# An MLP whose first quarter becomes like its others: two units of seven block products for eight, and a residual turned in four separate steps

## The chip, the core and the metric

One Trainium2 chip, one of its cores. The metric is the device time of one execution in microseconds, median of several runs; a run of the kernel before and one of the changed kernel are compared on the same chip.

## The reference

One layer of an encoder trunk on 256 tokens of width 2048, in float32: a mixer of retention and gated delta rule, a cross-attention, and an MLP of hidden width 8192. The change touches the MLP and what stands right before it:

```
x = x + cross_attention(h, mem_n, w_xq[l], w_xkv[l], w_xo[l])
h = rms_norm(x, norm_ffn_g[l])
x = x + jnp.square(jax.nn.relu(h @ w_ff1[l])) @ w_ff2[l]
return rms_norm(x, norm_final_g)
```

## The kernel before

Every large product is made of three matmuls. A float32 operand is split into a rounded part (the `whi` tiles, a cast on ScalarE, L125) and a remainder (`wlo`, a subtraction on VectorE, L126), and high by high, high by low and low by high are summed. Weights come through `fetch`: one transfer of 1 MB on SP's queue (L113) into one of three `raw` buffers, whose two halves of 1024 columns are then cast and get their remainders. The split halves live in three pairs of buffers, and every fourth half goes to a spare pair (`whx`, `wlx`) as soon as `spare` holds a pool. A scheduler sets the final order on each engine; every engine and SP's queue then run in that order.

The MLP runs in four quarters of 2048 hidden columns each (`fb`). A quarter first makes its hidden columns, eight groups (`b2`) of 256, each from two fetches of w_ff1 (numbered here 0 to 15, two to a group): 64 matmuls at L210 for a group. `evac_h` takes each group from PSUM, rectifies, squares and splits it. Then come the products with w_ff2 (L1227). A plain one takes a block of 512 by 512 weights for all 256 tokens, 24 matmuls. `with_seven` instead makes the product of 2 by 2 blocks with seven smaller products of 12 matmuls for eight: it loads the weight blocks b11, b12, b22, b21 (L1210, 1 MB each) into `rt` and `tr`, subtracts them from one another on VectorE (L1261, two halves of 1024 columns), and reads sums of hidden blocks that `token_sums` has made. Each finished product is added to the residual `res` on VectorE (L1142).

`rt` holds the residual with features on the partitions, and `res` needs it with tokens there. So VectorE transposes it in blocks of 32 by 32 into `tr` (L1124, four instructions of 1024 columns), and `place` copies it on into `res`: 32 transfers of 64 KB on SP's queue (L1131, called scatters here), in runs of 128 bytes. Each scatter needs all four transposes, and b22 and b21 can be loaded into `tr` only after all scatters.

A quarter's w_ff2 has 16 blocks of 512 by 512. Quarters two to four make eight of them as two such units of seven products (14 x 12 matmuls) and eight plain (8 x 24), and put some of the products between the last groups of hidden columns (`early`). The first makes one unit with seven (7 x 12) and twelve blocks plain (12 x 24), all of it after its hidden columns; its scatters go four to a group, all along the hidden columns. The norm ahead of the MLP has its own small matmuls (L1042); 54 matmuls of the first quarter stand before them.

Of the kernel before, what the change touches and what calls it, by code (L numbers as in the profile page):

```python
# [52 lines left out]
def trunk(ctx: ExitStack, tc: tile.TileContext, x_f, mem_f, positions, lead_f, small_f, w_in, ret_gn_g, w_out, w_xq,  # L53
# [23 lines left out]
    spare, turn = [], [0]  # L77
# [26 lines left out]
    def fetch(pieces, k, n, cuts=1, hold=None, at=(0, 0)):  # L104
# [3 lines left out]
        with tc.high_priority(offset=100000):  # L108
# [6 lines left out]
            for i in range(2):  # L115
# [1021 lines left out]
    spare.append(fp)  # L1137
# [60 lines left out]
    def with_seven(hid, rows, last, early):  # L1198
# [80 lines left out]
        if early:  # L1279
            load_block(b11, 0, 0)  # L1280
            yield
            load_block(b12, 0, 1)
            product(shared, part(0, 0), b11, "shared", (b11, b12, b11))
            read((0, 0, shared))
            yield
            load_block(b22, 1, 1)
            product(p5, summed(0), b11, "p5", (b11, b22, b11))
            read((1, 0, p5), (1, 1, p5))
            yield
            load_block(b21, 1, 0)  # L1290
            product(shared, summed(1), b11, "shared", (b12, b22, b12))
            read((1, 0, shared))
            yield
            product(shared, summed(2), b12, "shared", (b11, b21, b11))
            read((0, 1, shared), (1, 1, shared))
            if last:
                product(p5, summed(3), b22, "p3")
                read((1, 0, p5))
            yield
            for n in range(2):  # L1300
                take(n, stream_ps())
            plain(0, 2)
            load_block(b12, 0, 3)
            if last:
                final.append(quad_a().both.rearrange("p k s -> p (k s)").bitcast(F32))
                with tc.issue_after(fetched[-1]):
                    nc.sync.dma_start(final[0], norm_final_g.partition_broadcast(P))
            if not last:
                product(own[1][0], summed(3), b22, (1, 0))
            plain(0, 3)  # L1310
            load_block(b22, 1, 3)
            product(own[0][0], part(1, 0), b21, (0, 0))
            read((0, 0, own[0][0], True))
            product(own[0][1], part(1, 1), b11, (0, 1))
            read((0, 1, own[0][1], True))
            plain(1, 2)
            load_block(b11, 0, 2)
            take(2, [bank(), bank()])
            plain(2, 2)
            load_block(b21, 1, 2)  # L1320
            opened.difference_update(("shared", "p5"))
            product(shared, part(0, 0), b11, "shared", (b11, b12, b11))
            read((2, 0, shared))
            plain(1, 3)
            read(*((1, t, own[1][t], True) for t in range(NT)))
            product(p5, summed(0), b11, "p5", (b11, b22, b11))
            read((3, 0, p5), (3, 1, p5))
            plain(2, 3)
            take(3, stream_ps())
            product(own[3][0], summed(3), b22, (3, 0), (b12, b22, b12))  # L1330
            plain(3, 2)
            product(shared, summed(1), b11, "shared", (b11, b21, b11))
            read((3, 0, shared))
            if not last:
                plain(3, 3)
                read(*((3, t, own[3][t]) for t in range(NT)))
                product(own[2][0], part(1, 0), b21, (2, 0))
                read((2, 0, own[2][0]))
                product(shared, summed(2), b12, "shared")
                read((2, 1, shared), (3, 1, shared))  # L1340
                product(own[2][1], part(1, 1), b11, (2, 1))
                read((2, 1, own[2][1]))
            else:
                product(own[2][0], part(1, 0), b21, (2, 0))
                read((2, 0, own[2][0], True), (2, 1, own[2][1]))
                plain(3, 3, True)
                of_7 = parted(b12)
                with tc.issue_after(latest["lo"]), tc.issue_after(latest["hi"]):
                    add(3, 0, own[3][0])
                    of_4 = parted(b11, quad_b)  # L1350
                with tc.high_priority(offset=50000):
                    settle(3, 0)
                    latest["lo"] = latest["add"]
                    mean_square(0)
                    r_0 = factor(0)
                    finish(0, r_0, (0, 512, act, nc.sync), (1024, 1536, act, nc.sync))
                for those in unscaled:
                    scale(*those)
                read((3, 1, own[3][1]))
                product(shared, summed(2), None, "shared", halves=of_7)  # L1360
                read((3, 1, shared, True), (2, 1, shared))
                ends_of = stream_ps()
                product(ends_of, part(1, 1), None, "end", halves=of_4)
                with tc.high_priority(offset=50000):
                    with tc.issue_after(latest["square"]):
                        finish(0, r_0, (512, 1024, act, nc.sync), (1536, D, act, nc.sync))
                    junk = fp.tile([P, 2, S], F32, name="hs", tag="hs", bufs=2)
                    for c, ps in enumerate(ends_of):
                        with tc.issue_after(latest["lo"]):
                            got = add(2, 1, ps[:, :256], c * 256, c * 256 + 256)  # L1370
                        acc = ssq4[:, 1, 3 + c:4 + c]
                        vec.scalar_tensor_tensor(junk[:, c], got, 1.0, got, op0=ALU.mult, op1=ALU.mult, accum_out=acc)
                        if c:
                            vec.scalar_tensor_tensor(sums[1], acc, 1.0 / D, sums[1], op0=ALU.mult, op1=ALU.add)
                        else:
                            mean_square(1)
                    finish(1, factor(1), (0, 256, act, nc.sync), (512, 1024, vec, act), (256, 512, act, nc.sync),
                           (1024, 1536, vec, nc.sync), (1536, D, vec, act))
        else:
            for n in range(2):  # L1380
                take(n, stream_ps())
# [37 lines left out]
    for fb in range(4):  # L1419
# [5 lines left out]
        for b2 in range(8):  # L1425
# [17 lines left out]
            if early and b2 > 2:  # L1443
                next(parts_of)
# [46 lines left out]
```

## Time and profile before

| | |
|---|---|
| median of 3 runs | 2045.62 us (2044.28 to 2046.14) |
| span of the profiled execution | 2043.3 us; no other time of that execution is listed |
| TensorE busy | 2030.5 us, 99% |
| VectorE, ScalarE busy | 1550.6 us (76%), 1184.3 us (58%) |
| DMA queue of SP | 402.74 MB, 62.2% of 16 engines |

A span runs from the first instruction to the last. A wait is named by the instruction that waited and the one that released it. "DMA share" is the mean busy share of the core's 16 DMA engines; overlapping packets can bring it above 1.

### The profile page before, as it was taken

The numbers are of one execution on the slowest core, as the hardware profiler recorded it, in microseconds if no ns is written. First come the engines' busy times: TensorE is split into PE (matmuls) and PEld (weight loads), VectorE is DVE, ScalarE is ACT, GpSimd is POOL, SyncE is SP. The second block draws the span as 40 slices with busy tenths as digits, with TensorE's granted clock in tenths as the row PEclk, the third lists the DMA queues.
The fourth block names the chain that finished last, engine by engine and source line by source line (L and its number), as shares of the span: only waits on it lengthen the run. The fifth ranks groups of instructions, "written<-read, shape, count | busy, mean of one in ns | idle before, by whom it ended". The sixth has DMA issues, their size and how long they took to land.

```text
span 2043.3 us, 28453 instructions
## 1 busy us (share of the span) xinstructions
PE 2030.5 (99%) x10802; PEld 1751.4 (86%) x10802; DVE 1550.6 (76%) x2423; ACT 1184.3 (58%) x1941; POOL 38.7 (2%) x50
## 2 busy tenths in 40 slices
PE   9999999999999999999999999999999999999998
PEld 7888888988888888888888899888888888888886
DVE  5887788779667875888567666777867887888788
ACT  6655764575457554755446565555547656656655
POOL 0000000000000000000000000000000000000000
PEclk9999999999999999999999999999999999999999
DMA  9689556466555655555467655569657656665761
GB/s 329 209 259 303 184 185 197 154 189 201 180 166 183 198 190 165 186 181 190 156 212 244 191 183 163 174 180 254 221 168 234 219 163 214 201 204 166 242 231 62
DMA packets 329370, 405.24 MB, mean 198 GB/s; under 512 B 34944, under 2 KB 239632, under 8 KB 329104
## 3 DMA queue, kind: packets, MB, share of 16 engines
q1 hardware_dynamic: 328800, 402.74, 62.2%
q8 instruction: 84, 1.38, 0.3%
q10 hardware_dynamic: 432, 0.69, 0.1%
q14 instruction: 54, 0.44, 0.1%
HBM read 389.74 MB, written 11.55 MB: 196 GB/s over the span
## 4 chain that ended last, share of the span: by engine, by line
PE 97%; DVE 2%; issue 0%; DMA 0%; ACT 0%; SPq 0%; DVEq 0%; POOLq 0%; POOL 0%; ACTq 0%
PE s L210 52%; PE s L167 8%; PE s L168 8%; PE s L166 8%; PE b L1227 7%; PE s L1227 7%; PE s L400 1%; PE s L401 1%; PE s L402 1%; PE b L795 1%; PE b L698 1%; PE b L138 1%; PE b L828 1%; PE b L137 1%; PE b L139 1%
## 5 line engine op out<-in xcount | busy, mean ns | idle before, releaser
L210 PE MATMUL s<-q,whi 128*128 128x512 f32 x2816 | 969.0, 390 | 0.6 <-DVE bo L220 0.6
L126 DVE TENSOR_TENSOR wlo<-raw,whi 128x1024 fp32r<-128x1024 f32 x586 | 715.1, 1222 | 296.3 <-ACT whi L125 291.7
L125 ACT ACTIVATE whi<-raw 128x1024 fp32r<-128x1024 f32 x586 | 620.8, 1060 | 488.9 <-PE s L210 209.2
L210 PE MATMUL s<-q,wlo 128*128 128x256 f32 x2816 | 765.0, 281 | 0.0
L210 PEld LDWEIGHTS s<-q,whi 128*128 128x128 f32 x2816 | 520.6, 188 | 101.4 <-DVE bo L220 0.9
L210 PEld LDWEIGHTS s<-q,wlo 128*128 128x128 f32 x2816 | 527.2, 188 | 12.6 <-DVE wlo L126 0.5
L167 PE MATMUL s<-wlo,q 128*128 128x512 f32 x704 | 277.2, 394 | 0.0
L168 PE MATMUL s<-whi,q 128*128 128x512 f32 x704 | 274.9, 391 | 0.0
L166 PE MATMUL s<-whi,q 128*128 128x512 f32 x704 | 254.4, 391 | 0.0
L166 PEld LDWEIGHTS s<-whi,q 128*128 128x128 f32 x704 | 132.1, 188 | 27.4
L168 PEld LDWEIGHTS s<-whi,q 128*128 128x128 f32 x704 | 132.3, 188 | 26.2
L167 PEld LDWEIGHTS s<-wlo,q 128*128 128x128 f32 x704 | 132.3, 188 | 26.2
L219 ACT ACTIVATE bo<-s 128x256 f32<-128x256 f32 x192 | 73.2, 381 | 105.5 <-PE s L210 105.5
L220 DVE TENSOR_TENSOR bo<-bo,s 128x256 f32<-128x256 f32 x192 | 79.9, 416 | 43.0 <-ACT bo L219 42.8
L1227 PE MATMUL s<-whi,q 128*128 128x512 f32 x280 | 90.4, 389 | 0.0
L1250 DVE TENSOR_TENSOR wlo<-rt,whi 128x1024 fp32r<-128x1024 f32 x54 | 65.8, 1224 | 32.3 <-ACT whi L1249 31.6
L210 PE MATMUL s<-q,whx 128*128 128x512 f32 x256 | 89.2, 389 | 0.0
L125 ACT ACTIVATE whx<-raw 128x1024 fp32r<-128x1024 f32 x58 | 61.5, 1060 | 43.2 <-PE b L1227 17.2
L126 DVE TENSOR_TENSOR wlx<-raw,whx 128x1024 fp32r<-128x1024 f32 x58 | 70.9, 1222 | 17.9 <-ACT whx L125 17.4
L1249 ACT ACTIVATE whi<-rt 128x1024 fp32r<-128x1024 f32 x54 | 57.2, 1060 | 38.1 <-PE s L1227 17.8
L210 PE MATMUL s<-q,wlx 128*128 128x256 f32 x256 | 70.4, 280 | 0.0
L1227 PE MATMUL b<-whi,q 128*128 128x512 f32 x216 | 70.3, 389 | 0.0
(350 smaller groups left out, 2372.2 us busy)
## 6 DMA issues: line engine op xcount, KB each, us to landing
raw<-w_in SPq DMA_DIRECT2D x143, 1024.0 KB
raw<-w_ff SPq DMA_DIRECT2D x100, 1024.0 KB
raw<-w_xkv SPq DMA_DIRECT2D x29, 1024.0 KB
raw<-w_out SPq DMA_DIRECT2D x16, 1024.0 KB
raw<-w_xq SPq DMA_DIRECT2D x16, 1024.0 KB
raw<-w_xo SPq DMA_DIRECT2D x16, 1024.0 KB
rt<-w_ff SPq DMA_DIRECT2D x14, 1024.0 KB
tr<-w_ff SPq DMA_DIRECT2D x14, 1024.0 KB
```

The source lines that it names most:

```text
L125: latest["hi"] = act.activation(hi[:, cs], src[:, cs], AF.Copy).ins
L126: latest["lo"] = vec.tensor_sub(lo[:, cs], src[:, cs], hi[:, cs].bitcast(F32)).ins
L137: pe.matmul(o, lhs[0], rhs[0], start=first, stop=False)
L166: pe.matmul(o, xh, wh, start=first, stop=False)
L167: pe.matmul(o, xh, wl, start=False, stop=False)
L168: pe.matmul(o, xl, wh, start=False, stop=last)
L210: ins = pe.matmul(ps[b][:, :S] if part else ps[b], halves[h][part][:, i, b * P:(b + 1) * P], x[:, kk % 4, :], start=kk == 0 and not part, ...
L219: act.activation(o, ps[b][:, S:], AF.Copy)
L220: vec.tensor_add(o, o, ps[b][:, :S])
L1227: ins = pe.matmul(o, lhs[l], rhs[r], start=key not in opened, stop=last and j == 2, skip_group_check=True).ins
L1249: latest["hi"] = act.activation(hi, raw[:, c:c + 1024], AF.Copy).ins
L1250: latest["lo"] = vec.tensor_sub(lo, raw[:, c:c + 1024], hi.bitcast(F32)).ins
```

## The change

The first quarter takes the way of the others: `with_seven` loses its `early` switch and the other branch, `evac_h` rectifies and squares on ScalarE. The four transposes are put into a list, and `fetch` takes one out behind each remainder, after four empty entries. The scatters move: none in groups 0, 6 and 7, eight in groups 1 to 3, four in groups 4 and 5. The spare pair of buffers is handed out after group 0, and `sv` is then allocated before it. The long block under `if early:` only loses its indentation.

```
     fetched, steps, latest = [], [], {}
-    spare, turn = [], [0]
+    spare, turn, turns = [], [0], []
...
                     latest["lo"] = vec.tensor_sub(lo[:, cs], src[:, cs], hi[:, cs].bitcast(F32)).ins
+                if turns:
+                    turn_round_next = turns.pop(0)
+                    with tc.issue_after(latest["lo"]):
+                        turn_round_next()
...
-    for c in range(4):
+
+    def turn_round(c):
         vec.transpose(*(a[:, 4 * c:4 * c + 4, :].rearrange("p k s -> p (k s)") for a in (tr, rt)))
+
+    turns.extend(4 * [lambda: None] + [lambda c=c: turn_round(c) for c in range(4)])
...
-    spare.append(fp)
...
-    def with_seven(hid, rows, last, early):
+    def with_seven(hid, rows, last):
...
-        early = fb > 0
-        parts_of = with_seven(hid, rows, fb == 3, early)
+        parts_of = with_seven(hid, rows, fb == 3)
...
-                if early:
-                    act.activation(ps, ps, AF.Relu)
-                    act.activation(hs[:, b, :], ps, AF.Square)
-                else:
-                    vec.scalar_tensor_tensor(hs[:, b, :], ps, 0.0, ps, op0=ALU.max, op1=ALU.mult)
+                act.activation(ps, ps, AF.Relu)
+                act.activation(hs[:, b, :], ps, AF.Square)
...
-            blocks(h3, w_ff1[0], fb * D + b2 * 256, 2, evac_h, ends if early else None)
-            if early and b2 > 2:
+            blocks(h3, w_ff1[0], fb * D + b2 * 256, 2, evac_h, ends)
+            if fb == 0:
+                if b2 == 0:
+                    spare.append(fp)
+                for b8 in ((), (0, 1), (2, 3), (4, 5), (6,), (7,), (), ())[b2]:
+                    place(b8)
+            if b2 > 2:
                 next(parts_of)
-            if fb == 0:
-                place(b2)
```

On TensorE the first quarter keeps its 512 matmuls at L210, and its 372 at L1227 become 360 (L1233 in the changed kernel).

SP's queue before, from the first fetches of w_ff1 (`raw<-w_ff`, two to a group; `res<-tr` are scatters, `rt<-w_ff` loads of w_ff2 blocks):

```order
L113 DMA raw<-w_ff 128x8x256 x5
L1131 DMA res<-tr 32x16x32 x2
L113 DMA raw<-w_ff 128x8x256
L1131 DMA res<-tr 32x16x32 x3
L113 DMA raw<-w_ff 128x8x256
L1131 DMA res<-tr 32x16x32 x4
L113 DMA raw<-w_ff 128x8x256
L1131 DMA res<-tr 32x16x32 x7
L113 DMA raw<-w_ff 128x8x256 x2
L1131 DMA res<-tr 32x16x32 x4
```

Three more pairs of fetches follow, each with four scatters behind it, and only then the loads of w_ff2. The same place of the queue now:

```order
L113 DMA raw<-w_ff 128x8x256 x7
L1138 DMA res<-tr 32x16x32 x5
L113 DMA raw<-w_ff 128x8x256
L1216 DMA rt<-w_ff 128x4x512
L1138 DMA res<-tr 32x16x32 x4
L113 DMA raw<-w_ff 128x8x256
L1138 DMA res<-tr 32x16x32 x7
L113 DMA raw<-w_ff 128x8x256
L1216 DMA rt<-w_ff 128x4x512
L1138 DMA res<-tr 32x16x32 x6
L113 DMA raw<-w_ff 128x8x256
L1138 DMA res<-tr 32x16x32 x6
```

Fetch 11, four more scatters, fetch 12 and the load of b22 into `tr` come next. So the 32 scatters stand between fetch 6 and fetch 12, with the loads of b11 and b12 among them.

VectorE before, where the transposes stand (`wlo`, `wlx` are remainders of halves of weights, `n_s` is the norm):

```order
L126 TENSOR_TENSOR wlo<-raw,whi 128x1024 x2
L1044 TENSOR_SCALAR n_s<-b 128x2
L1124 STREAM_TRANSPOSE tr<-rt 128x1024 x4
L126 TENSOR_TENSOR wlx<-raw,whx 128x1024
L1115 TENSOR_TENSOR rstd3q<-n_r 128x2
```

The `wlx` there is the second half of fetch 1, which TensorE takes up behind fetch 2. And now, where `wlx` and the `wlo` after it are the two halves of fetch 3:

```order
L126 TENSOR_TENSOR wlo<-raw,whi 128x1024 x2
L1129 STREAM_TRANSPOSE tr<-rt 128x1024 x2
L1048 TENSOR_SCALAR n_s<-b 128x2
L126 TENSOR_TENSOR wlx<-raw,whx 128x1024
L1129 STREAM_TRANSPOSE tr<-rt 128x1024
L224 TENSOR_TENSOR bo<-bo,s_13013 128x256
L126 TENSOR_TENSOR wlo<-raw,whi 128x1024
L1129 STREAM_TRANSPOSE tr<-rt 128x1024
```

The four stand apart, the last one two remainders later than before.

VectorE of the changed kernel around the second of the early products (`L1256` splits b11, `L1267` subtracts b22, which is in `tr`, from it; the last row is the first remainder of fetch 12):

```order
L1256 TENSOR_TENSOR wlo<-rt,whi 128x1024
L1256 TENSOR_TENSOR wlx<-rt,whx 128x1024
L1267 TENSOR_TENSOR rt<-tr,rt 128x1024
L1148 SCALAR_TENSOR_TENSOR res<-b,rstd3q,res 128x512
L1267 TENSOR_TENSOR rt<-tr,rt 128x1024
L126 TENSOR_TENSOR wlo<-raw,whi 128x1024
```

Before, the first quarter has no such rows among its hidden columns; its products come after fetch 15.

## Rows read from the trace of the kernel before

**Rows 1.** The page: span, TensorE, and groups (busy us, mean ns, idle before).

```profile
span 2043.3 us, 28453 instructions
...
PE 2030.5 (99%) x10802; PEld 1751.4 (86%) x10802; DVE 1550.6 (76%) x2423; ACT 1184.3 (58%) x1941; POOL 38.7 (2%) x50
...
L126 DVE TENSOR_TENSOR wlo<-raw,whi 128x1024 fp32r<-128x1024 f32 x586 | 715.1, 1222 | 296.3 <-ACT whi L125 291.7
L125 ACT ACTIVATE whi<-raw 128x1024 fp32r<-128x1024 f32 x586 | 620.8, 1060 | 488.9 <-PE s L210 209.2
```

**Rows 2.** Waits of TensorE, whole span: us in total, times, longest.

```profile
PE s L210 <- DVE bo L220: 0.6, 1, 0.6
```

**Rows 3.** Timeline of TensorE: start, duration, instruction, [idle before <- releaser].

```profile
1367.93 0.28 PE L210 MATMUL s<-q,wlx 128*128 128x256 f32 x1
1368.79 0.50 PE L210 MATMUL s<-q,whi 128*128 128x512 f32 x1 [0.58 <-DVE bo L220]
```

**Rows 4.** Stretches, all engines: first quarter after the norm, second quarter.

```profile
1357.84:1522.74 164.90, 164.32 (x832) 139.87 (x832) 125.47 (x163) 82.34 (x103) 0.70 (x1) 1.00 0.74 213
1522.74:1692.74 170.00, 170.00 (x873) 145.73 (x872) 137.05 (x164) 103.63 (x144) 0.00 (x0) 1.00 0.61 196
```

**Rows 5.** Stretch, line 210 alone, third quarter: PE, PEld, PEclk, DMA, GB/s.

```profile
1693.27:1863.38 170.11, 89.13 (x512) 78.46 (x512) 1.00 0.61 198
```

**Rows 6.** Stretches, line 1227 alone, first and second quarter.

```profile
1438.30:1522.80 84.50, 84.43 (x372) 69.70 (x372) 1.00 0.52 177
1522.70:1693.00 170.30, 82.37 (x360) 67.29 (x360) 1.00 0.61 196
```

**Rows 7.** Timeline of VectorE around the transposes.

```profile
1357.67 1.22 DVE L126 TENSOR_TENSOR wlo<-raw,whi 128x1024 fp32r<-128x1024 f32 x1 [1.26 <-ACT whi L125]
...
1358.88 4.61 DVE L1124 STREAM_TRANSPOSE tr<-rt 128x1024 f32<-128x1024 f32 x4
1363.42 1.18 DVE L126 TENSOR_TENSOR wlx<-raw,whx 128x1024 fp32r<-128x1024 f32 x1
```

**Rows 8.** Groups by line in the second quarter: busy us, mean ns.

```profile
L1261 DVE TENSOR_TENSOR rt<-tr,rt 128x1024 f32<-128x1024 f32 x12 | 14.2, 1218 | 0.0
...
L1142 DVE SCALAR_TENSOR_TENSOR res<-b,rstd3q,res 128x512 f32<-128x512 f32 x13 | 9.4, 745 | 0.2 <-PE b L1227 0.2
```

**Rows 9.** Timeline of SP's queue, start and duration of issues, first quarter.

```profile
1356.44 0.37 SPq L113 DMA_DIRECT2D raw<-w_ff  x1
1363.57 1.40 SPq L1131 DMA_DIRECT2D res<-tr  x2
...
1375.21 1.08 SPq L113 DMA_DIRECT2D raw<-w_ff  x1
1376.34 8.64 SPq L1131 DMA_DIRECT2D res<-tr  x7
1385.07 1.20 SPq L113 DMA_DIRECT2D raw<-w_ff  x2
...
1393.47 3.20 SPq L113 DMA_DIRECT2D raw<-w_ff  x2
...
1411.92 2.59 SPq L113 DMA_DIRECT2D raw<-w_ff  x2
1414.56 6.90 SPq L1131 DMA_DIRECT2D res<-tr  x4
```

**Rows 10.** Stretches, all engines; the last three numbers are PEclk, DMA share, GB/s.

```profile
1381.50:1385.00 3.50, 3.50 (x21) 3.07 (x21) 1.30 (x3) 1.76 (x4) 0.00 (x0) 1.00 1.07 99
1397.50:1400.50 3.00, 3.00 (x20) 2.63 (x19) 2.97 (x7) 1.49 (x4) 0.00 (x0) 1.00 1.06 349
1413.00:1415.00 2.00, 2.00 (x13) 1.78 (x12) 0.10 (x1) 0.31 (x1) 0.00 (x0) 1.00 0.35 68
1427.00:1443.00 16.00, 16.00 (x88) 13.82 (x88) 10.69 (x17) 8.70 (x14) 0.00 (x0) 1.00 1.05 388
```

**Rows 11.** The stretch of all scatters, all engines.

```profile
1365.00:1424.00 59.00, 58.42 (x337) 51.17 (x336) 45.07 (x79) 31.26 (x49) 0.00 (x0) 1.00 1.01 232
```

**Rows 12.** The stretch after the issue of a single fetch, all engines.

```profile
1356.50:1358.00 1.50, 1.50 (x12) 1.38 (x12) 0.33 (x1) 1.06 (x1) 0.00 (x0) 1.00 0.21 58
```

**Rows 13.** Timeline of ScalarE: a cast that waited for its fetch.

```profile
1391.75 1.06 ACT L125 ACTIVATE whi<-raw 128x1024 fp32r<-128x1024 f32 x1 [4.14 <-DMA raw<-w_ff]
```

More of the change, by code (lines that the diff above doesn't have):

```diff
@@ new lines, in with_seven @@
+        load_block(b11, 0, 0)
+        yield
+        load_block(b12, 0, 1)
+        product(shared, part(0, 0), b11, "shared", (b11, b12, b11))
+        read((0, 0, shared))
+        yield
+        load_block(b22, 1, 1)
+        product(p5, summed(0), b11, "p5", (b11, b22, b11))
+        read((1, 0, p5), (1, 1, p5))
+        yield
+        load_block(b21, 1, 0)
+        product(shared, summed(1), b11, "shared", (b12, b22, b12))
+        read((1, 0, shared))
+        yield
+        product(shared, summed(2), b12, "shared", (b11, b21, b11))
@@ new lines, in with_seven @@
+        read((0, 1, shared), (1, 1, shared))
+        if last:
+            product(p5, summed(3), b22, "p3")
+            read((1, 0, p5))
+        yield
+        for n in range(2):
+            take(n, stream_ps())
+        plain(0, 2)
+        load_block(b12, 0, 3)
+        if last:
+            final.append(quad_a().both.rearrange("p k s -> p (k s)").bitcast(F32))
+            with tc.issue_after(fetched[-1]):
+                nc.sync.dma_start(final[0], norm_final_g.partition_broadcast(P))
@@ new lines, in with_seven @@
+        if not last:
+            product(own[1][0], summed(3), b22, (1, 0))
+        plain(0, 3)
+        load_block(b22, 1, 3)
+        product(own[0][0], part(1, 0), b21, (0, 0))
+        read((0, 0, own[0][0], True))
+        product(own[0][1], part(1, 1), b11, (0, 1))
+        read((0, 1, own[0][1], True))
+        plain(1, 2)
+        load_block(b11, 0, 2)
+        take(2, [bank(), bank()])
+        plain(2, 2)
+        load_block(b21, 1, 2)
+        opened.difference_update(("shared", "p5"))
@@ new lines, in with_seven @@
+        product(shared, part(0, 0), b11, "shared", (b11, b12, b11))
+        read((2, 0, shared))
+        plain(1, 3)
+        read(*((1, t, own[1][t], True) for t in range(NT)))
+        product(p5, summed(0), b11, "p5", (b11, b22, b11))
+        read((3, 0, p5), (3, 1, p5))
+        plain(2, 3)
+        take(3, stream_ps())
+        product(own[3][0], summed(3), b22, (3, 0), (b12, b22, b12))
+        plain(3, 2)
+        product(shared, summed(1), b11, "shared", (b11, b21, b11))
+        read((3, 0, shared))
@@ L1430, in evac_h @@
             def evac_h(b, ps):
-                if early:
-                    act.activation(ps, ps, AF.Relu)
-                    act.activation(hs[:, b, :], ps, AF.Square)
-                else:
-                    vec.scalar_tensor_tensor(hs[:, b, :], ps, 0.0, ps, op0=ALU.max, op1=ALU.mult)
+                act.activation(ps, ps, AF.Relu)
+                act.activation(hs[:, b, :], ps, AF.Square)
                 qh, ql = (a[:, b2 % 2 * 2 + b, :] for a in hid[-1])
```

177 lines of the change are left out of this document (44 added, 133 removed).

## The prediction, made before the change had run

> **What bounds the kernel now.** I read the page first. TensorE is busy 2030.5 of 2043.3 us [rows 1], so the question is what it does in that time and where the 13 us are. The list of waits gives one TensorE wait after the start of the kernel: 0.6 us for a PSUM evacuation [rows 2]. The timeline puts it at 1367.93, where one matmul starts 0.86 us after the one before it [rows 3]; that is in the first quarter of the MLP, which the change rewrites. Next I cut the MLP at its quarters. The second takes 170.00 us with TensorE busy for all of it; the first takes, from the norm to its end, 164.90 us, of which 0.58 idle [rows 4]. 54 of its matmuls run before the norm, at 0.174 us (89.13 us over 512 [rows 5]), so the first quarter takes 164.9 + 9.4 = 174.3 us. The granted clock is 1.00 in all of these, its 2.4 GHz level. An instruction that leaves TensorE's queue shortens the kernel, and one that arrives too late lengthens it.
>
> **What the change takes away.** The second kind of matmul (L1227) drops from 372 to 360 in the first quarter, as many as the others have. They stand at 84.43 us for 372 and 82.37 for 360 [rows 6], 2.1 us apart; 12 times 84.43/372 = 0.227 us gives 2.7. The stall at 1367.93 goes too: the half of fetch 1 that used the spare buffer waited behind the four transposes (4.61 us in one piece, its remainder after them at 1363.42 [rows 7]), so the first group of hidden columns ended late and its PSUM banks were freed late. With the spare buffer given out one group later, halves are used in their order. If the new first quarter ran like the second, it would take 170.0 us for 174.3: **-4.3 us**, of which 2.7 are the matmuls, 0.6 the stall, and 1.0 short delays and slower pairs around it.
>
> **What it adds off TensorE.** Six more halves of a weight block are cast (1.06 us on ScalarE) and get their remainder (1.222 on VectorE) [rows 1], eight more 1024-column subtractions (1.218) and six more additions into the residual (0.745) come to VectorE [rows 8], and 16 squares go from VectorE to ScalarE. VectorE: 7.3 + 9.7 + 4.5, 21.5 us, less the squares. I cost this at nothing: the second quarter has the same instructions, with VectorE busy 137.05 and ScalarE 103.63 of its 170.00 us (before, the first has 125.47 and 82.34), and TensorE has no gap there [rows 4]. Without that cover each us would count. The spare buffer also moves in SBUF, by the 2 KB of another tile; no row gives that a price, and I take nothing.
>
> **The transposes.** One by one, the fourth ends later. Up to the remainder that starts at 1357.67 the order is as before, so it ends at 1358.9; then come two transposes (1.15 each), the norm's short step, a remainder 1.2, a transpose, an addition (some 0.4), a remainder 1.2 and the last transpose [rows 7]: 1366.4, for 1363.5 before. The remainder ahead of it ends at 1365.2 and is needed by TensorE at about 1365.3, so 0 to 0.5 us; I take 0. But the 32 scatters need all four transposes, and start 2.9 us later.
>
> **The transfers.** Before, the 32 scatters lie between 1363.57 and 1421.46 on SP's queue, among eleven fetches [rows 9]. Now they lie among six, with two loads of w_ff2 squeezed in, and everything behind them on the queue waits. Prices: in 1381.5 to 1385, where nearly only scatters move, the engines are full (share 1.07) at 99 GB/s, so 65.5 KB take 0.66 us; fetches move at 349 GB/s, 1048.6 KB in 3.0; loads at 388, 2.7 [rows 10]. Check on before: 1365 to 1424 moved 232 GB/s x 59 us = 13.7 MB [rows 11]; less 32 scatters (2.10 MB) that is 11.06 fetches, so 33.2 + 21.1 = 54.3 of 59 us. 4.7 us are lost; 1.3 of them are in 1413 to 1415 (share 0.35 [rows 10]), where a fetch waited for its buffer [rows 9], and about 1 is the start. That leaves 4%.
>
> Now the queue of the changed kernel. Fetch 6 waits for the remainder that ends at 1365.2; its bytes flow 1.3 to 1.8 us after its issue (the one issued at 1356.44 had moved 87 KB by 1358.0 [rows 9, 12]); with 1.8, from 1367.1. Up to the end of fetch 11 stand six fetches, two loads and 28 scatters: 18.0 + 5.4 + 18.5 = 41.9, with 4% 43.6 us: 1410.7. Software sees it about 1.2 us later (the fetch issued at 1385.07 released ScalarE at 1391.75, and could be over at 1390 to 1391 [rows 9, 13]); cast and remainder take 1.06 + 1.22: 1414.2. TensorE, if never stopped, needs it at 1412.3: 1357.84, plus 10 matmuls of fetch 1, eight fetches of 5.53, one product of 2.75, fetch 10, and one matmul. **Stall 1.9.** Then the second product: its subtraction takes b22, whose load stands behind four more scatters and fetch 12: 1410.7 + (2.6 + 3.0 + 2.7) x 1.04 + 1.2 = 1420.5. VectorE runs in order, and the first remainder of fetch 12 stands behind that subtraction, an addition to the residual and a second subtraction: 1.22 + 0.75 + 1.22 + 1.22 = 4.4, so 1424.9; it is due at 1412.1 + 5.53 + 2.75 + 0.23 + 1.9 = 1422.5. **Stall 2.4.** Later fetches have slack, since no scatter is left and each group of columns now shares its time with a product. Sum: -4.3 + 4.3 = 0.0 on the profiled execution's span of 2043.3 us; what lies around it (the median is 2.3 us above that span) stays, so **2045.6**.
>
> With nothing lost between transfers fetch 11 ends at 1409.0 and the stalls are 0.2 and 2.1: 2043.6. With 8% lost they are 3.6 and 2.7: 2047.6.
>
> **Rivals.** (1) *The transfers are hidden.* For it: before, with the engines full for 59 us, TensorE lost only 0.58 us to a wait, and that one was not a transfer's. Against: then 58 us held eleven fetches and 32 scatters, and now 45 us must hold six, two loads and 28. No stall: 2045.6 - 4.3 = 2041.3. The same comes out if a scatter cost what its bytes cost at a load's rate, 0.17 us: 28 then take 4.7 instead of 18.5, and everything is early by 13 us. Against that stand the 99 GB/s at full share [rows 10]; I give this way 0.04 of the 0.22 below. The Trainium skill's page "DMA: Bandwidth & Descriptors", in "Why small descriptors are slow (HBM only)", says that transfers between SBUF and SBUF don't suffer from small descriptors, and that 128-byte packets still reach 78% of the link; the scatters are such transfers. By that rule the stalls would vanish; the trace disagrees.
>
> (2) *Long groups of scatters cost more; the kernel is slower.* From the fetch at 1375.21 to that at 1385.07 the queue spent 9.86 us on a fetch and seven scatters [rows 9]: 0.98 for each scatter. If the groups of 7, 6 and 6 pay that, 19 x 0.32 = 6.1 us take the place of the 1.7 lost in the sum, fetch 11 comes 4.4 us later, and nothing behind absorbs it: 2050.0. It decides from 0.97 us for a scatter in these groups (4.1 us more). Against: a cycle of two fetches and four scatters took 8.4 us (1385.07 to 1393.47), 0.6 for each.
>
> (3) *The transposes stop TensorE*: the remainder due at 1365.3 comes 1 us late or more, 2046.5 and up.
>
> **Numbers.** Chances: the forecast, 2043.6 to 2047.6, 0.54; (1) 0.22; (2) 0.18; (3) or another wait 0.06. 0.2% is 4.1 us, about what a measurement of this kernel can tell from no change. (1) lies on that bound, so I count two thirds of it as faster: 0.15; of (2) three quarters as slower, with some of (3): 0.16; same 0.69. The range takes in (1) and (2): 2041.2 to 2050.2; the forecast's own is 2043.6 to 2047.6.
>
> **What would show it.** TensorE's 360 matmuls and the lost wait at 1368 are the first step. For the second, TensorE's idle time lies where fetch 11 and fetch 12 start, some 55 and 64 us after the norm, ScalarE waiting for a transfer ahead of the first, VectorE for b22's load ahead of the second, with the share of the DMA engines near 1 from the first scatter on. No idle time there shows (1); idle time from fetch 9 on shows (2). A quarter that is longer than 170 us without idle time would show that my cover for VectorE and ScalarE, or the buffers' places, is wrong.

## The result

The changed kernel takes 2051.19 us (median of 6 runs, 2049.99 to 2052.68) against 2045.3 before (6 runs): ratio 1.0027, 95% interval 1.0017 to 1.0037, some 5.9 us slower. A second set of runs gave 2050.88 (7 runs), 1.0028 (1.0017 to 1.0039). The forecast was 2045.6, no change, with a range up to 2050.2.

The page after, against [rows 1] (its parts 1 and 4, the span first):

```profile
span 2051.0 us, 28478 instructions
...
PE 2032.9 (99%) x10790; PEld 1751.8 (85%) x10790; DVE 1562.5 (76%) x2427; ACT 1201.7 (59%) x1979; POOL 39.6 (2%) x50
...
PE 93%; DVE 2%; DMA 2%; SPq 1%; issue 1%; ACT 0%; DVEq 0%; POOLq 0%; POOL 0%; ACTq 0%
```

VectorE and ScalarE are a little busier. What is to be seen is in the last line, the chain of work that ended last: two shares that don't belong to a kernel bound by TensorE, DMA 2% and SP's queue 1%. The list of TensorE's waits from the norm on (us in total, times, longest) says what came in place of the one PSUM wait of [rows 2]:

```profile
PE s L214 <- ACT whi L125: 3.4, 2, 1.9
PE s L214 <- DVE wlo L126: 1.7, 3, 0.8
```

Casts and remainders of weights come late, 5.1 us in five waits. The timeline of TensorE has four of them (the bracket is the idle time and what ended it):

```profile
1359.56 0.50 PE L1046 MATMUL b<-ones,acc 128*128 128x2 f32 x4
...
1411.64 0.74 PE L214 MATMUL s<-q,whi 128*128 128x512 f32 x2 [1.50 <-ACT whi L125]
1412.91 0.39 PE L214 MATMUL s<-q,wlo 128*128 128x256 f32 x1 [0.52 <-DVE wlo L126]
...
1420.15 0.50 PE L214 MATMUL s<-q,whi 128*128 128x512 f32 x1 [1.88 <-ACT whi L125]
1421.41 0.56 PE L214 MATMUL s<-q,wlo 128*128 128x256 f32 x1 [0.77 <-DVE wlo L126]
1421.78 0.63 PE L214 MATMUL s<-q,whi 128*128 128x512 f32 x1
...
1422.42 0.63 PE L214 MATMUL s<-q,whi 128*128 128x512 f32 x1
```

The first row, the norm's matmuls, gives the offset: they stand at 1359.56, and at 1357.48 in the execution of before. The program ahead of them is the same, and in the runs below they lie anywhere between 1356.7 and 1359.6, so these 2.1 us aren't the change's; times of this trace are 2.1 later than the prediction's. From the norm to the end the kernel takes 691.4 us, for 685.8 before: +5.6. The waits belong to fetch 10 (1411.64 and 1412.91) and fetch 11 (1420.15 and 1421.41); the fifth, 0.44 us at 1432.26, to fetch 12. The last two rows are a pair of matmuls apart: 0.64 us, where a pair took 0.345. ScalarE's timeline says what the casts waited for:

```profile
1410.54 1.06 ACT L125 ACTIVATE whi<-raw 128x1024 fp32r<-128x1024 f32 x1 [3.24 <-DMA raw<-w_ff]
...
1419.05 1.06 ACT L125 ACTIVATE whi<-raw 128x1024 fp32r<-128x1024 f32 x1 [5.96 <-DMA raw<-w_ff]
```

ScalarE stood idle until the fetch landed, so no work of its own made it late. SP's queue from fetch 6 on, against [rows 9] (left out: fetches 7 to 9 and the loads of b11 and b12):

```profile
1367.06 0.37 SPq L113 DMA_DIRECT2D raw<-w_ff  x1
1368.26 4.89 SPq L1138 DMA_DIRECT2D res<-tr  x5
...
1374.49 6.24 SPq L1138 DMA_DIRECT2D res<-tr  x4
...
1383.13 8.20 SPq L1138 DMA_DIRECT2D res<-tr  x7
...
1392.66 10.88 SPq L1138 DMA_DIRECT2D res<-tr  x6
1403.65 0.57 SPq L113 DMA_DIRECT2D raw<-w_ff  x1
1404.26 6.35 SPq L1138 DMA_DIRECT2D res<-tr  x6
1410.71 1.40 SPq L113 DMA_DIRECT2D raw<-w_ff  x1
1412.15 4.70 SPq L1138 DMA_DIRECT2D res<-tr  x4
```

Read the second column: SP issues almost without a pause (its fetches' waits for free buffers between 1373 and 1417 sum to 1.7 us; before, between 1363 and 1422, to 9.4). The six groups of scatters hold it for 41.3 us, 1.29 us for each scatter, and a fetch is issued right behind the last of its group. The stretches of that time show the engines meanwhile (the last three numbers are the granted clock, the share and GB/s):

```profile
1368.00:1378.00 10.00, 10.00 (x60) 8.69 (x59) 8.72 (x17) 7.72 (x16) 0.00 (x0) 1.00 0.97 209
1378.00:1388.00 10.00, 10.00 (x59) 8.69 (x58) 7.67 (x15) 5.98 (x11) 0.00 (x0) 1.00 1.01 269
1388.00:1398.00 10.00, 10.00 (x58) 8.66 (x57) 4.00 (x7) 3.79 (x6) 0.00 (x0) 1.00 0.86 184
1398.00:1408.00 10.00, 9.97 (x56) 8.40 (x55) 7.18 (x13) 7.49 (x13) 0.00 (x0) 1.00 0.81 176
1408.00:1418.00 10.00, 7.98 (x42) 6.25 (x40) 5.66 (x7) 2.55 (x4) 0.00 (x0) 1.00 0.97 205
...
1402.00:1404.00 2.00, 2.00 (x13) 1.73 (x13) 2.00 (x5) 1.90 (x4) 0.00 (x0) 1.00 0.35 47
...
1406.00:1408.00 2.00, 2.00 (x12) 1.68 (x12) 1.97 (x5) 1.10 (x2) 0.00 (x0) 1.00 0.85 233
...
1421.00:1426.00 5.00, 4.58 (x18) 3.96 (x19) 4.34 (x6) 4.17 (x9) 0.00 (x0) 0.66 1.03 356
```

The first five have a mean share of 0.92 and 209 GB/s; before it was 1.01 and 232 [rows 11]. The next two are from one cycle: the scatters of the group are through, fetch 10 was issued only at 1403.65, and the share climbs from 0.35 to 0.85 over 6 us. The last has the granted clock at 0.66: after 1.88 and 0.77 us of idle TensorE ran, as I estimate from that mean, some 3.4 of 5 us at its 1.2 GHz level, and lost 1.7.

### The profile page after: what moved, and what is told of

It is laid out like the page before. It is cut to its first block, busy times and chain, and to the rows that moved or that the text cites. A ratio compares the mean times of both kernels' runs of the same rounds, so it can differ in the third digit from the quotient of the medians.

```text
span 2051.0 us, 28478 instructions
## 1 busy us (share of the span) xinstructions
PE 2032.9 (99%) x10790; PEld 1751.8 (85%) x10790; DVE 1562.5 (76%) x2427; ACT 1201.7 (59%) x1979; POOL 39.6 (2%) x50
## 4 chain that ended last, share of the span: by engine, by line
PE 93%; DVE 2%; DMA 2%; SPq 1%; issue 1%; ACT 0%; DVEq 0%; POOLq 0%; POOL 0%; ACTq 0%
PE s L214 49%; PE s L171 8%; PE s L172 8%; PE s L170 8%; PE s L1233 7%; PE b L1233 6%; SPq L1138 1%; PE s L404 1%; PE s L405 1%; PE s L406 1%; PE b L799 1%; DVE wlo L126 1%; PE b L142 1%; PE b L832 1%; PE b L141 1%
## 5 line engine op out<-in xcount | busy, mean ns | idle before, releaser
L214 PE MATMUL s<-q,whi 128*128 128x512 f32 x2824 | 973.4, 391 | 3.4 <-ACT whi L125 3.4
L126 DVE TENSOR_TENSOR wlo<-raw,whi 128x1024 fp32r<-128x1024 f32 x599 | 729.9, 1221 | 293.0 <-ACT whi L125 288.9
L125 ACT ACTIVATE whi<-raw 128x1024 fp32r<-128x1024 f32 x599 | 634.9, 1061 | 510.7 <-PE s L214 210.1
L214 PE MATMUL s<-q,wlo 128*128 128x256 f32 x2824 | 767.3, 281 | 2.2 <-DVE wlo L126 2.2
L214 PEld LDWEIGHTS s<-q,whi 128*128 128x128 f32 x2824 | 522.6, 188 | 105.2 <-ACT whi L125 4.1
L214 PEld LDWEIGHTS s<-q,wlo 128*128 128x128 f32 x2824 | 529.4, 188 | 16.7 <-DVE wlo L126 4.2
L171 PE MATMUL s<-wlo,q 128*128 128x512 f32 x704 | 277.2, 394 | 0.0
L172 PE MATMUL s<-whi,q 128*128 128x512 f32 x704 | 274.9, 391 | 0.0
L170 PE MATMUL s<-whi,q 128*128 128x512 f32 x704 | 254.4, 391 | 0.0
L170 PEld LDWEIGHTS s<-whi,q 128*128 128x128 f32 x704 | 132.1, 188 | 27.4
L172 PEld LDWEIGHTS s<-whi,q 128*128 128x128 f32 x704 | 132.3, 188 | 26.2
L1233 PE MATMUL s<-whi,q 128*128 128x512 f32 x384 | 122.1, 389 | 0.0
L1256 DVE TENSOR_TENSOR wlo<-rt,whi 128x1024 fp32r<-128x1024 f32 x55 | 67.3, 1224 | 33.5 <-ACT whi L1255 33.1
L214 PE MATMUL s<-q,whx 128*128 128x512 f32 x248 | 86.6, 390 | 0.0
L1233 PEld LDWEIGHTS s<-whi,q 128*128 128x128 f32 x384 | 72.1, 188 | 15.0
L1233 PE MATMUL s<-wlo,q 128*128 128x512 f32 x192 | 74.7, 389 | 0.0
L214 PE MATMUL s<-q,wlx 128*128 128x256 f32 x248 | 68.2, 280 | 0.0
L1233 PE MATMUL b<-whi,q 128*128 128x512 f32 x208 | 67.2, 389 | 0.0
```

The costliest lines, as they stand in the source:

```text
L170: pe.matmul(o, xh, wh, start=first, stop=False)
L171: pe.matmul(o, xh, wl, start=False, stop=False)
L172: pe.matmul(o, xl, wh, start=False, stop=last)
L214: ins = pe.matmul(ps[b][:, :S] if part else ps[b], halves[h][part][:, i, b * P:(b + 1) * P], x[:, kk % 4, :], start=kk == 0 and not part, ...
L1233: ins = pe.matmul(o, lhs[l], rhs[r], start=key not in opened, stop=last and j == 2, skip_group_check=True).ins
L1256: latest["lo"] = vec.tensor_sub(lo, raw[:, c:c + 1024], hi.bitcast(F32)).ins
```

## The experiments

Ratios are to the kernel before on the same chip, with the 95% interval; medians of before were 2045.6 to 2046.1. A trace shows one execution; those of the runs with 64 and with 16 evenly placed scatters and with the transposes in one piece (2054.12, 2046.93 and 2044.91 us) are 1.9 to 3.2 us below the medians of their runs. So medians say how much, and traces where the waits are.

### Runs of 2 KB in place of 128 bytes

```
-    to = res[b8 % 4 * 32:b8 % 4 * 32 + 32, b8 // 4, :].rearrange("i (k a f) -> i k a f", a=4, f=32)[:, :, a, :]
-    nc.sync.dma_start(to, tr[32 * a:32 * a + 32, :, b8 * 32:b8 * 32 + 32])
+    to = res[b8 % 4 * 32:b8 % 4 * 32 + 32, b8 // 4, a * 512:a * 512 + 512].rearrange("i (k s) -> i k s", s=S)
+    nc.sync.dma_start(to, tr[32 * a:32 * a + 32, 2 * b8:2 * b8 + 2, :])
```

> The changed kernel with each of the 32 scatters replaced by a copy of the same 64 KB in runs of 2 KB (the residual's rows then hold the wrong elements). Theory, scatters fill SP's queue: a copy should cost about its bytes at the loads' 388 GB/s, 0.17 us instead of 0.7 to 1.1, so fetches 10 and 11 come early, TensorE's waits between 1409 and 1422 and the low clock behind them vanish, and 2042 to 2044 us come out. Rival A, each transfer costs its 0.7 to 1 us on the queue whatever its runs: 2050 to 2051. Rival B, the loss comes from the added work on VectorE and ScalarE: 2049 to 2051.

2042.84 us, 0.9984 (0.9976 to 0.9993). TensorE has no wait left in the first quarter. First its stretch 1366 to 1418, then the shortest, median and longest issue of a scatter in ns, before (`L1131`), in the changed kernel and in this one:

```profile
1366.00:1418.00 52.00, 52.00 (x294) 45.15 (x293) 41.25 (x65) 34.69 (x60) 0.00 (x0) 1.00 1.02 294
```

```profile
L1131 SPq DMA_DIRECT2D res<-tr x32: 591/1341/3317, 1363.6 to 1419.4; - x32
L1138 SPq DMA_DIRECT2D res<-tr x32: 592/1016/3487, 1368.3 to 1415.4; - x32
L1138 SPq DMA_DIRECT2D res<-tr x32: 507/589/2054, 1359.9 to 1399.8; - x32
```

Rival B falls: all of the work added on VectorE and ScalarE is here. Rival A falls too: the same number of transfers now mostly holds SP for 0.59 us each, and the engines move 294 GB/s. The first row of the three says something else: a scatter held SP as long before the change. One caution: a copy also needs only one of the four transposes, so the first ones start earlier than the scatters did, 2.6 us after the norm for 8.7, and eight of them stand ahead of fetch 6. Part of the gain can be that start (a run below changes it alone).

### The products a group later

```
-            if b2 > 2:
+            if b2 > (2 if fb else 3):
                 next(parts_of)
...
-                for b8 in ((), (0, 1), (2, 3), (4, 5), (6,), (7,), (), ())[b2]:
+                for b8 in ((), (0, 1), (2,), (3, 4), (5,), (6,), (7,), ())[b2]:
```

> The changed kernel with the first quarter's products and loads one group of hidden columns later, and its scatters spread over groups 1 to 6. Same work, same number of matmuls. Theory, scatters fill SP's queue: some 5 us more for the same transfers ahead of fetch 11, so most of the 7 us of waits and low clock go: 2043 to 2046. Rival B, added work on VectorE and ScalarE: 2049 to 2052, since all of that work is still there.

A miss: 2052.96 us, 1.0036 (1.0022 to 1.0050). The edit made a wait of its own. TensorE's timeline of this run, then VectorE's:

```profile
1455.58 0.76 PE L1233 MATMUL b<-whi,sh 128*128 128x512 f32 x1 [4.72 <-DVE res L1148]
```

```profile
1449.82 1.22 DVE L1256 TENSOR_TENSOR wlx<-rt,whx 128x1024 fp32r<-128x1024 f32 x1
1450.96 2.35 DVE L1267 TENSOR_TENSOR rt<-tr,rt 128x1024 f32<-128x1024 f32 x2
...
1453.56 1.22 DVE L126 TENSOR_TENSOR wlo<-raw,whi 128x1024 fp32r<-128x1024 f32 x1
1454.69 0.74 DVE L1148 SCALAR_TENSOR_TENSOR res<-b,rstd3q,res 128x512 f32<-128x512 f32 x1
```

The third and fourth product now follow each other on TensorE, both into the bank `shared`. The fourth has to wait until the third is added into `res`, and that addition stands behind the fourth's remainder, two subtractions and a fetch's remainder on VectorE. A wait for a fetch also stayed, 2.22 us at 1408.10 and 0.76 behind it, 3.0 us for 4.7 at fetches 10 and 11 in the changed kernel: the later products cured less than was expected. The rise in time is the new wait's; the added VectorE work is hidden only while hidden columns or a plain product stand between two products. The next edit puts one there.

### The same, with a plain product between

```
         for n in range(2):
             take(n, stream_ps())
         plain(0, 2)
         product(shared, summed(2), b12, "shared", (b11, b21, b11))
```

in the first quarter, where the plain product stood behind that product.

> The first quarter's products one group later, with a plain product between the third and the fourth, but with the 32 scatters of 64 KB, in the same places as in the run with the later products alone. The wait of 4.7 us and the low clock behind it (some 6 us) go; the one at 1405 for a fetch behind b11's load and six scatters stays, some 3 us: 2045.5 to 2048. If the later products alone cured everything, the width of the scatters counting for nothing: 2042.5 to 2044.5.

2046.24 us, 1.0006 (0.9998 to 1.0015). The wait between the products is gone; a wait for a fetch stays, 1.37 us at 1407.44 and 0.76 at 1408.70, with its low clock. More time ahead of b22 cures a part, not all.

### Scatters on ScalarE's queue

```
-                nc.sync.dma_start(to, tr[32 * a:32 * a + 32, :, b8 * 32:b8 * 32 + 32])
+                nc.scalar.dma_start(to, tr[32 * a:32 * a + 32, :, b8 * 32:b8 * 32 + 32])
```

> The changed kernel with the scatters issued from ScalarE's queue instead of SP's. Theory as it stands (the fetch waits behind scatters in the order of one queue): fetches 8 to 11 are issued early and share the engines with the scatters; 2043 to 2048. If instead the 16 engines themselves are what is short, fetches move slower by what scatters take, and b22 is as late as before: 2048 to 2051. ScalarE may also be held up by its own issues: above 2051.

2053.73 us, 1.0039 (1.0026 to 1.0051), the last of the three cases. ScalarE's list of waits in 1364 to 1410 ("issue" is time in which nothing in the profile held it but its own queue's issues):

```profile
ACT bo L1399 <- issue: 4.9, 3, 2.7
ACT whi L125 <- issue: 3.3, 3, 2.2
```

The longest issue in its timeline:

```profile
1375.36 3.65 ACTq L1138 DMA_DIRECT2D res<-tr  x1
```

An issue holds the engine that makes it, and the casts behind it come late. The Trainium skill ("Perfetto Trace Analysis", "DMA Optimizations") says that where descriptor generation is the bottleneck, spreading transfers over several issuing engines may help. Here it moved the wait onto an engine whose time counts. For the theory this run says more than its time does. Its stretch 1366 to 1418:

```profile
1366.00:1418.00 52.00, 45.83 (x238) 37.72 (x236) 31.38 (x54) 28.45 (x50) 0.00 (x0) 0.97 1.09 239
```

The same 32 scatters, from another queue, leave the engines full (1.09 and 239 GB/s, for the 0.94 and 207 of the changed kernel below), and from 1364 to 1430 no cast waits for a fetch, where in the changed kernel such waits take 17.5 us. How early the fetches came isn't told, since ScalarE was late itself.

### Half and twice the number of transfers

The transposes write `tr` so that token halves and features have one stride, and 16 scatters of 128 KB, still in runs of 128 bytes, do the work of 32.

```
-        vec.transpose(*(a[:, 4 * c:4 * c + 4, :].rearrange("p k s -> p (k s)") for a in (tr, rt)))
+        vec.transpose(tr.rearrange("p k s -> p (k s)").rearrange("p (t k s) -> p k t s", t=NT, s=P)[:, 4 * c:4 * c + 4, :, :],
+                      rt[:, 4 * c:4 * c + 4, :].rearrange("p k (t s) -> p k t s", t=NT))
...
+    to = res[b * 32:b * 32 + 32, :, :].rearrange("i t (k a f) -> i (t k) a f", a=4, f=32)[:, :, a, :]
+    at = tr[32 * a:32 * a + 32, :, :].rearrange("i k s -> i (k s)").rearrange("i (tk b f) -> i tk b f", b=4, f=32)[:, :, b, :]
+    nc.sync.dma_start(to, at)
```

> The changed kernel with its 32 scatters of 64 KB made into 16 of 128 KB, in the same runs of 128 bytes; the transposes write their columns in another order for it, and the bytes of each group stay. Theory by now, SP's queue runs dry: behind each group of scatters the next fetch is issued only when they are nearly through (each transfer holds SP for 0.6 us or more), and the engines' share falls to 0.2 to 0.8 for some 3 us in each cycle. With half as many transfers the fetches are issued earlier and most of that comes back: 2043 to 2047. Rival, the runs of 128 bytes cost engine time: as many packets as before, so 2049 to 2052.

2049.84 us, 1.0016 (1.0007 to 1.0025): in the rival's range. But in this run the first two groups held 5 and 4 wide scatters ahead of fetch 8, twice the bytes of the changed kernel, and fetches 8 and 9 were late instead. So the next run fixes the places, fetch by fetch:

```
+            for n, _ in enumerate(blocks_in_steps(h3, w_ff1[0], fb * D + b2 * 256, 2, evac_h, ends)):
+                if fb == 0 and n % 2 == 0:
+                    for _ in range({5: 3, 7: 2, 8: 3, 9: 3, 10: 3, 11: 2}.get(2 * b2 + n // 2, 0)):
+                        place(*moves.pop(0))
```

> The changed kernel with 16 scatters of 128 KB, now placed so that about the same bytes stand between the same fetches as in it (3, 2, 3, 3, 3 and 2 for 5, 4, 7, 6, 6 and 4 of half the size). In the run with wide scatters the first two groups were twice as many bytes, so it did not part the two. Theory, the queue runs dry because each group is many small transfers ahead of a fetch: the engines' share between 1368 and 1420 goes from 0.92 towards 1.0, and most of TensorE's waits between 1409 and 1422 go: 2044 to 2047. Rival, 128-byte runs beside fetches make the engines themselves slow: waits as in the changed kernel, 2049.5 to 2052.

2048.85 us, 1.0014 (1.0005 to 1.0023), between the two ranges. Beside it, on the same chip, the changed kernel itself:

> The changed kernel once more, beside the three others on the same chip: 2050 to 2052, with TensorE waiting for the casts of fetches 10 and 11.

2050.88 us, 1.0028 (1.0017 to 1.0039). The intervals of 16 and 32 scatters overlap, though six of the seven single times with 32 lie above all eleven with 16. And the other way, 64 scatters of 32 KB, about the same bytes between the same fetches:

```
+            nc.sync.dma_start(to[:, k:k + 8, :], tr[32 * a:32 * a + 32, k:k + 8, b8 * 32:b8 * 32 + 32])
...
+                    for _ in range({5: 10, 7: 8, 8: 14, 9: 12, 10: 12, 11: 8}.get(2 * b2 + n // 2, 0)):
```

> The changed kernel with 64 scatters of 32 KB in the same runs of 128 bytes, about the same bytes between the same fetches (5 of them one fetch earlier). Theory, the number of transfers on SP's queue counts: the time ahead of a fetch grows with the number, the engines' share from 1366 to 1418 falls below 0.94, TensorE waits longer for fetches 9 to 11: 2054 to 2064. Rival, bytes and runs alone count: 2049 to 2052.

2057.31 us, 1.0057 (1.0044 to 1.0071). The stretch 1366 to 1418 of each, with 64 scatters, with 32 (the changed kernel, second set) and with 16:

```profile
1366.00:1418.00 52.00, 45.64 (x243) 38.13 (x242) 33.50 (x57) 28.86 (x54) 0.00 (x0) 0.96 0.74 175
```

```profile
1366.00:1418.00 52.00, 47.81 (x263) 40.13 (x261) 33.02 (x55) 28.46 (x51) 0.00 (x0) 1.00 0.94 207
```

```profile
1366.00:1418.00 52.00, 50.27 (x280) 42.68 (x279) 36.19 (x60) 31.92 (x58) 0.00 (x0) 1.00 1.03 225
```

And SP's timeline, one group of 384 KB behind fetch 9, with 64 and with 16 scatters:

```profile
1390.50 12.69 SPq L1137 DMA_DIRECT2D res<-tr  x12
```

```profile
1391.14 7.47 SPq L1140 DMA_DIRECT2D res<-tr  x3
```

Same bytes, same runs: 175, 207 and 225 GB/s at a share of 0.74, 0.94 and 1.03. That group of 384 KB holds SP for 12.7, 10.9 (the row at 1392.66 above) and 7.5 us. The number of transfers on the queue counts. With 64 it counts in a second way, which neither other run has; SP's waits in 1366 to 1422:

```profile
SPq L1137 <- DMA raw<-w_ff: 8.5, 5, 2.5
```

Each is a scatter that waits until a fetch has landed which stands eight transfers ahead of it on the queue; 2.5 of the 12.7 us are such a wait. So the step from 32 to 64 isn't the hold of the issues alone; the one from 32 to 16 is free of this. In the run with 16, the waits for fetch 10 (1.35 and 0.52 us in the changed kernel here) shrank to 0.53 and those for fetch 11 (2.27 and 0.71) to 0.44 and 0.76; SP now waited for a free buffer again, 4.6 us for one fetch, where in 1373 to 1417 of the changed kernel its longest wait was 0.8.

### The subtraction with b22

With fetches 10 and 11 nearly in time, the wait that the prediction had put at fetch 12 grew from 0.44 us to 2.0. TensorE and then VectorE in the run with 16 evenly placed scatters:

```profile
1426.50 0.50 PE L214 MATMUL s<-q,wlo 128*128 128x256 f32 x2 [2.04 <-DVE wlo L126]
```

```profile
1422.30 1.22 DVE L1269 TENSOR_TENSOR rt<-tr,rt 128x1024 f32<-128x1024 f32 x1 [1.64 <-DMA tr<-w_ff]
1423.44 0.74 DVE L1150 SCALAR_TENSOR_TENSOR res<-b,rstd3q,res 128x512 f32<-128x512 f32 x1
1424.10 1.22 DVE L1269 TENSOR_TENSOR rt<-tr,rt 128x1024 f32<-128x1024 f32 x1
1425.23 1.22 DVE L126 TENSOR_TENSOR wlo<-raw,whi 128x1024 fp32r<-128x1024 f32 x1
```

VectorE waits for b22's load, and subtraction, addition, subtraction stand ahead of fetch 12's remainder, in the order that the prediction gave. The second product doesn't itself read what that subtraction makes, so it can stand later:

```
-        product(p5, summed(0), b11, "p5", (b11, b22, b11))
+        product(p5, summed(0), b11, "p5", None if first else (b11, b22, b11))
         read((1, 0, p5), (1, 1, p5))
         yield
+        if first:
+            ...
+                        vec.tensor_sub(*(v[:, c:c + 1024] for v in (b11, b22, b11)))
```

> The run with 16 scatters in the places of the changed kernel's, with the subtraction that needs b22 moved on VectorE behind the remainders of fetch 13. By the prediction's step on b22 the wait near 1425 (2.0 us idle, with its low clock or short delays up to 3) goes and nothing takes its place: 2046 to 2047.5. If the third product is then late instead, as late by as much: 2048 to 2050.

2046.39 us, 1.0005 (0.9996 to 1.0013). The wait at fetch 12 is gone; one of 1.16 us came at 1441.41, a group further on, for a remainder. About half of the idle time came back there; the time against before went from +3.1 to +0.8 us, with intervals that overlap, so the wait's going is shown by the trace and the size of the gain is not.

### The other steps alone

The transposes one by one and the spare buffers a group later, on the kernel before (`turns` and `turn_round` as in the change, scatters in groups 1 to 7):

> The kernel before with only the transposes one by one behind remainders and the spare buffers a group later; its scatters have to start one group later (eight in group 1, then four to a group), everything else is as before. By the first step of the prediction the wait of 0.6 us at 1367.93 goes, with up to 1.0 of short delays: 2043.7 to 2045. Rival, the transposes and the shifted buffers are what costs: 2047 or more. If the eight scatters in group 1 already make fetches late, 2045 to 2047 with TensorE waiting for a fetch.

2044.70 us, 0.9994 (0.9985 to 1.0003): not told apart from no change by time. In the trace the PSUM wait of [rows 2] is gone, no other came, and from the norm to the end it takes 684.5 us for 685.8.

The four transposes in one piece, on the changed kernel:

```
-    turns.extend(4 * [lambda: None] + [lambda c=c: turn_round(c) for c in range(4)])
+    for c in range(4):
+        turn_round(c)
```

> The changed kernel with the four transposes in one piece as before. The prediction took the transposes at nothing and had the scatters start 2.9 us later by them. If that start is what counts, fetches 10 and 11 come up to 2.9 us earlier, against a wait of about 0.7 us near 1368: 2047.5 to 2050. If the order of the transfers behind it matters more than their start: 2050 to 2053.

2047.85 us, 1.0010 (1.0001 to 1.0019), about 3 us less than the changed kernel. The scatters start at 1363.4, 6.1 us after the norm instead of 8.7; fetch 10's waits are 0.84 and 0.52, fetch 11's none, and the one for the late remainder is 0.25.

Squares back on VectorE in the first quarter:

```
+                if fb == 0:
+                    vec.scalar_tensor_tensor(hs[:, b, :], ps, 0.0, ps, op0=ALU.max, op1=ALU.mult)
```

> The changed kernel with the first quarter's rectifying and squaring back on VectorE (one instruction for two on ScalarE). The prediction took the added work on both engines at nothing. By that and by the theory that transfers are late: 2050 to 2052, as the changed kernel. If ScalarE's load made casts late: 2047 to 2050. If VectorE is the one without room: above 2052.

2049.96 us, 1.0019 (1.0010 to 1.0028), on the border of the first two cases. Not slower than the changed kernel, with 4.7 us of waits for 5.1; the intervals overlap, so no gain is claimed either. Where the squares stand decides nothing that these runs can tell.

### A faster version

Later products, a plain product between the third and the fourth, wide scatters (in groups 1 to 6):

> The 16 scatters of 128 KB, and the first quarter's products one group of hidden columns later, with a plain product put between the third and the fourth product of seven (in the run with the later products TensorE waited 4.7 us there, for an addition that stood late on VectorE). Theory: no fetch is late, no wait between the products: 2041.5 to 2044. Rival, the added VectorE work costs by itself: a wait of some us at the products or in the plain products behind them, 2045 or more.

2043.28 us, 0.9986 (0.9978 to 0.9995), no wait of TensorE in the first quarter, 235 GB/s in 1366 to 1418. And with the transposes in one piece:

> The fastest kernel so far with the reference's outputs (later products, wide scatters), with the four transposes in one piece, so that the scatters start some 3 us earlier. By the theory no fetch was late there any more, so an earlier start gives nothing, and the transposes cost a wait of 0.3 to 0.7 us near 1366: 2042.5 to 2044. A wait there may also bring TensorE's pairs of matmuls from 0.353 us back to 0.345 us, as in the other run with one piece, over some 130 pairs: about 1 us less, 2042 to 2043.

2042.54 us, 0.9987 (0.9978 to 0.9996). Both beat both kernels; between the two the intervals decide nothing. The one wait left is 0.25 us, for a remainder at 1367.68. The matmuls at L214 in 25 us of this run, and of the one with 2 KB runs:

```profile
1370.00:1395.00 25.00, 25.00 (x147) 22.18 (x146) 1.00 1.09 251
```

```profile
1370.00:1395.00 25.00, 25.00 (x143) 21.72 (x142) 1.00 1.08 298
```

Four matmuls more in the same time, with no wait in either: see the last section.

## Why the prediction was wrong, step by step

**What bounds the kernel, what the change takes away: right, but 1 us too much.** With no transfer late, the runs end 2.8 to 3.2 us below before, not 4.3. The 12 matmuls and the PSUM wait are gone from the traces; their 2.7 and 0.6 us fit, though no run measures the 2.7 by itself. The 1.0 of "short delays and slower pairs" isn't there: in the new order the pairs are slower themselves from the norm to the first wait or product (143 matmuls for 147 in 25 us, so by estimate some 1.2 us over the 45 us up to the first product), where in the kernel before they were so for only 4 us behind the norm.

**Added VectorE and ScalarE work at nothing: right.** The runs without a wait do all of it. The cover is needed, though: where two products met, the wait was 4.7 us.

**The transposes at nothing on TensorE: right.** The last of the four on VectorE, against [rows 7]:

```profile
1366.95 1.23 DVE L1129 STREAM_TRANSPOSE tr<-rt 128x1024 f32<-128x1024 f32 x1
```

It ends at 1368.2, which is 1366.1 on the clock of before (1366.4 was forecast), and no wait stands there: rival 3 falls. Their price is the later start of the scatters, which the sum had taken in through fetch 6; undoing it gave 3 us back.

**The transfers: this step failed.** "That leaves 4%": I costed a scatter by what its bytes take with the engines full, 0.66 us, and carried over the 4% that before lost between transfers. The 10.2 MB of fetches 6 to 11 and what stands among them were to take 43.6 us, 234 GB/s. They moved at 209: from the issue of fetch 6 to the cast of fetch 11 the forecast had 46.7 us (1365.2 to 1411.9), and it took 52.0 (1367.06 to 1419.05). The engines weren't full throughout. SP was: it had issued fetch 11 only 43.7 us after fetch 6, 36.6 of them with 28 scatters, and fetch 11 took another 8.3 to its cast. So at the end of a group the engines had little left to move while the next fetch was only starting. [rows 9] had that price in rows of its own (7 scatters in 8.64 us, 1.23 each; 4 in 6.90, 1.73 each), and I used the first for the rival only. Nothing made a scatter dearer: before, its issue took 1.34 us at the median. But there its queue had slack, 9.4 us of waits for free buffers and eleven fetches' time to hide in, and now 28 scatters stood among six fetches and two loads. The sizes: TensorE lost 2.0 us to fetch 10, which I had in time, 2.65 to fetch 11 (forecast 1.9), 0.44 to fetch 12 (forecast 2.4), and 1.7 to the low clock behind them, which I hadn't in the sum at all. Together: -2.7 for the matmuls and -0.6 for the old wait, +5.1 idle, +1.7 clock and some +1.0 for slower pairs make 4.5 of the 5.6 us from norm to end. The first matmuls behind a wait (0.50 and 0.56 us in the rows above, for 0.39 and 0.28) are a part of the other 1.1; the rest isn't accounted for.

**b22's subtraction: the mechanism was right**, and the size too where it could show (2.04 for 2.4). In the changed kernel the earlier waits had moved TensorE back far enough to hide most of it.

**The rivals.** (2) had the row that decides (0.98 against a point of 0.97) and its time, 2050.0, was 1.2 us off; in two cycles a scatter cost 1.09 (fetch to fetch 10.6 us less 3.0, over 7; 12.2 less 3.0 and 2.7, over 6). Its reason, long groups, isn't the one shown: the number of transfers is, at the same bytes. What it had against it, 0.6 us in groups of four, was misread: two fetches went off a cycle of 8.4 us at 3.0 each, the time of their bytes, but they held SP for 1.2 together [rows 9], and the four scatters for nearly all of the rest. (1), no transfer late, is what the runs with 2 KB runs and with later products and wide scatters show. The Trainium skill's rule behind it ("DMA: Bandwidth & Descriptors", "Why small descriptors are slow (HBM only)": no penalty between SBUF and SBUF; its figure is from one remote transfer of 1 MB) would have made the run with 2 KB runs equal to the changed kernel but for its earlier start; it was 0.4% faster, and an issue took 0.59 us at the median for 1.02. The trace disagrees with the rule here.

**Left open.** What an issue of a scatter waits for. The same 64 KB held SP for 0.59 to 3.49 us. The two stretches of 10 us with a share of 0.86 and 0.81 might suggest that it is slow while the engines have room, but they average over both kinds. The longest issue and a short one, as stretches:

```profile
1394.94:1398.43 3.49, 3.49 (x22) 3.02 (x21) 0.33 (x1) 0.00 (x0) 0.00 (x0) 1.00 0.96 313
1402.91:1403.54 0.63, 0.63 (x5) 0.58 (x4) 0.63 (x3) 0.60 (x2) 0.00 (x0) 1.00 0.11 12
```

The long one stands while the engines move fetch 9, the short one when they have run down. That fits an issue of 0.6 us which beyond that waits for the engines to take it, so that SP never gets far ahead of them; no row names what released it, so this is argued and not shown.

## What to carry to other kernels

Price a small transfer by how long it holds its queue (from one issue to the next in the densest group of the trace), not by its bytes at the engines' rate; a queue with slack has the same hold and hides it. When a row gives a rival a price just past its turning point, that row belongs in the sum. And a gain of a few us from fewer matmuls can be eaten by what the new order asks of a queue: widen or spread the transfers first (16 for 32, the products a group later), and the gain comes, here 2.8 to 3.2 us.

## What the runs showed of the hardware that was not expected

- An issue occupies its engine: 0.6 us at least (0.59 for 32, 64 and 128 KB alike), 1.3 on the mean for 64 KB in runs of 128 bytes, up to 3.65 on ScalarE, where it delayed casts.
- A wait costs more than itself: after 1.88 and 0.77 us of idle the granted clock was 0.66 over 5 us, 1.7 us more. In the run with 16 even scatters, waits of 2.04 and 0.76 us were followed by no lower clock (1.00 from 1406 to 1430).
- TensorE's pairs of matmuls (512 and 256 columns) have two paces at the same granted clock of 1.00: 143 and 147 matmuls in 25 us. In the changed kernel the slower one begins at the norm's matmuls and stays until a wait or a product; in the run with one piece a wait of 0.25 us ended it. In the kernel before it ended by 1362.8 with neither, so a wait isn't needed. What makes it isn't known.
